# First attention of a two-layer trunk: norms of queries and keys over two token tiles, values straight from PSUM

## The chip, the cores and the metric

The kernel runs on one core of one Trainium2 chip. The metric is device microseconds of one execution, as the median of several runs: 2759.04 us for the kernel before (three runs, 2758.87 to 2761.37). The engines are named as the profile names them: PE is TensorE (matmuls; PEld its weight loads), DVE VectorE, ACT ScalarE, POOL GpSimd, and SP issues the DMAs.

## The reference, cut to what matters

Two transformer layers over 1024 latent tokens and 256 context tokens, model width 1024, 16 heads of 64. Layer 0 mixes by two-dimensional neighbourhood attention (the first attention), layer 1 by a sliding window with four key heads (the second attention); each layer ends with a gated feed-forward network. The change touches the norm of each head's query and key:

```python
def rmsnorm(x, g):
    x32 = x.astype(jnp.float32)
    y = x32 * lax.rsqrt(jnp.mean(x32 * x32, axis=-1, keepdims=True) + RMS_EPS)   # RMS_EPS = 1e-6
    return (y * g.astype(jnp.float32)).astype(x.dtype)

def attn_inputs(h, w_qkv, g_q, g_k, n_kv, with_q=True):
    y = h @ w_qkv
    q = rmsnorm(y[..., :D_MODEL].reshape(bsz, t, n_kv, N_HEADS // n_kv, HEAD_DIM), g_q)
    kv = y[..., D_MODEL:]
    k = rmsnorm(kv[..., :kv_w].reshape(bsz, t, n_kv, HEAD_DIM), g_k)   # over each head's 64 values
    v = kv[..., kv_w:].reshape(bsz, t, n_kv, HEAD_DIM)                 # not normed
    return q, k, v

def attend(q, k, v, bias=None, mask=None, sink=None):
    s = jnp.einsum('...qngd,...knd->...ngqk', q, k).astype(jnp.float32) * (HEAD_DIM ** -0.5)
    ...                                                                # + bias, mask; softmax p
    return jnp.einsum('...ngqk,...knd->...qngd', p.astype(v.dtype), v)
```

## The kernel before

The tokens lie in ten tiles of 128 (eight latent, two context). The first attention goes through eight head pairs. For each pair, `plan_na_qkv` (line 1084) plans one step per token tile, ten steps: eight groups of three matmuls give 384 columns in a PSUM bank `mm`: two heads of queries, two of keys, two of values. ScalarE copies all 384 columns to SBUF (`qraw`). `plan_rstd` (line 470) then makes the reciprocal root of the mean square of each of the four heads: ScalarE squares 256 columns (`qsq`), VectorE sums each head's 64 (`qv`), VectorE divides by 64 and adds the epsilon, GpSimd raises the four numbers to the power -1/2 (`qy`), and three small VectorE operations (`qt`, `qt`, `qy`) are a Newton step. VectorE scales queries and keys by it (`qn`). The values are copied from `qraw` by ScalarE or VectorE (`v`). Behind every second tile TensorE transposes the scaled queries and keys of both tiles (`pt<-idr,qn`), and ScalarE and VectorE split them in a high and a low part (`q`, `kkl`, `kll`; `kkc`, `klc` for the context).

`plan_na_su` plans the attention units on these: scores `s` on TensorE, a negated minimum with bias on VectorE (`S`, `m`), the exponential on ScalarE, the reciprocal of the sum (`sm`) and a scaling, transposes (`pt<-idr,S`) with copies back (`pt`), and the product with the values (`pv`, copied out as `osb`). The output projection of layer 0 follows (`woraw`, `whi`, `wlo` are its weights, `o2c`, `o0`, `o1` the split attention outputs, `oacc` its sums). The second attention (`plan_sw_qkv`, `plan_sw_ctx`) uses the same `plan_rstd`, with five and four heads a tile, and multiplies by rotary tables on VectorE or GpSimd (`qa`, `qb`).

The order on every engine is made by `Sched`. Each step is given to it with engines and an assumed duration, what it reads and writes, a key (earlier keys first), and which buffers it takes (`acq`) and gives back (`rel`). It plays the engines forward in time with these assumed durations and, whenever an engine is free, starts the ready step with the lowest key whose buffers are free; a step with two engines goes to the one that would finish it first. The instructions are then issued in that order, and on the chip each engine keeps it, waiting wherever an input is late. So a step that disappears, or another assumed duration, moves steps far from it, on every engine. The queries of pair `n` have the key `n`, the attention units `n + 5.5`; that is the distance by which projections run ahead. Two banks hold projections (`mm`), two `qraw` buffers.

All operations issued through this helper carry line 51 in the profile, so rows are told apart by the tiles that they write and read.

Of the kernel before, what the change touches and what calls it, by code (L numbers as in the profile page):

```python
# [11 lines left out]
F32 = mybir.dt.float32  # L12
# [5 lines left out]
P = 128  # L18
# [205 lines left out]
def trunk_kernel(ctx, tc, xtok, xseq, cc, crow, wmod, wmodt, bmod, gnorm, na_wqkv, na_gqk, na_bias, na_wo,  # L224
# [228 lines left out]
    def plan_qkv_mm(sc, key, psa, h, tt, slabs, s, J, c0=0, hkey=None):  # L453
# [3 lines left out]
        for kt in range(KT):  # L457
            def mm(e, kt=kt):
# [3 lines left out]
                for i, (a, w) in enumerate(((hh, wh), (hl, wh), (hh, wl))):  # L462
# [5 lines left out]
                  acq=[("mm", J["id"] + ("acc",), 1)] if kt == 0 else (), rel=[("w", i)] if kt % 2 else ())  # L468

    def plan_rstd(sc, key, J, c0, nh, wk, nsq):  # L470

        I = J["id"]

        def sq(e):
            J["sq"] = wk.tile([P, nsq], F32, tag="qsq", name="qsq", bufs=PTB["qsq"])
            act.activation(J["sq"][:, :nh * DH], J["raw"][:, c0:c0 + nh * DH], AF.Square)
        sc.op("act", t_act(nh * DH), sq, reads=[I + ("raw",)], writes=[I + ("sq",)], key=key, acq=[("qsq", I + ("sq",), 1)])

        def red(e):
            v = J["ms"] = tiny.tile([P, 5], F32, tag="qv", name="qv", bufs=4)  # L480
            dve.tensor_reduce(out=v[:, :nh], in_=J["sq"][:, :nh * DH].rearrange("p (h d) -> p h d", d=DH), axis=AX.X,
                              op=ALU.add)
        sc.op("dve", t_dve(nh * DH), red, reads=[I + ("sq",)], writes=[I + ("ms",)], key=key, rel=[I + ("sq",)])
# [6 lines left out]
        def pw(e):  # L490
            J["y"] = tiny.tile([P, 5], F32, tag="qy", name="qy", bufs=4)
            J["t"] = tiny.tile([P, 5], F32, tag="qt", name="qt", bufs=4)
            pool.tensor_tensor(out=J["y"][:, :nh], in0=J["ms"][:, :nh], in1=mhalf[:, :nh], op=ALU.pow)
        sc.op("pool", 0.42 + nh * 0.165, pw, reads=[I + ("ms",)], writes=[I + ("y",)], key=key)
        ny = lambda: (J["y"][:, :nh], J["t"][:, :nh], J["ms"][:, :nh])

        def newton(i):
            def f(e):
                y, t, v = ny()
                if i == 0:  # L500
                    dve.tensor_tensor(out=t, in0=y, in1=y, op=ALU.mult)
                elif i == 1:
                    dve.scalar_tensor_tensor(out=t, in0=t, scalar=-0.5, in1=v, op0=ALU.mult, op1=ALU.mult)
                else:
                    dve.scalar_tensor_tensor(out=y, in0=t, scalar=1.5, in1=y, op0=ALU.add, op1=ALU.mult)
# [3 lines left out]

# [543 lines left out]
    SBUFS, PTB = 5, dict(pt5=6, pt2=4, qsq=2)  # L1053
# [31 lines left out]
    def plan_na_qkv(n):  # L1085
# [7 lines left out]
        plan_qkv_mm(sc, key, psa, h, tt, slabs, hp, J, 0, ("h0", tt // 4) if hp == 0 else None)  # L1093

        def cp(e):
            J["raw"] = wk.tile([P, 384], F32, tag="qraw", name="qraw", bufs=2)
            act.activation(J["raw"], J["acc"][:, :384], AF.Copy)
        sc.op("act", t_actp(384), cp, reads=[K("acc")], writes=[K("raw")], key=key, acq=[("qraw", K("raw"), 2)],
              rel=[K("acc")])
# [1570 lines left out]
```

## Time and profile before

| | before |
|---|---|
| median of three runs | 2759.04 us (2758.87 to 2761.37) |
| span of the profiled execution | 2755.5 us, 42708 instructions |
| the profiled execution's own time | its span; the page gives none beyond it. The median is 3.5 us longer |
| PE / DVE / ACT / POOL busy | 2701.9 / 2247.1 / 1684.9 / 340.2 us |
| mean granted TensorE clock | 0.993 |
| first attention, projections and units | about 48 to 635 us |
| second attention | about 1620 to 2020 us |

Busy time is that of the records: matmul records overlap, so a TensorE that is busy throughout can still be waiting a little inside. The idle time of an engine is put down to what released it. The chain of waits follows the last instruction back to what released each step, and a share of it is time in which the end hung on that engine.

### The profile page before, as it was taken

The page shows a single profiled execution, that of the slowest core. Times are in us where ns is not written, and L with a number is a line of the kernel's source. Part 1 is how long each engine was busy: PE and PEld are TensorE (multiplying, and loading weights), DVE is VectorE, ACT ScalarE, POOL GpSimd, SP SyncE. Part 2 cuts the span into 40 slices and gives each one's busy share as a digit, 9 for nine tenths or more (in the row PEclk, how much of TensorE's full clock was granted, in tenths as well). Part 3 has the DMA queues.
Part 4 walks back from the last instruction along what each step waited for, and adds up shares of the span by engine and source line. Part 5 has one row for each costly group of instructions (what it writes and reads, how often), then busy time and mean ns, then how long its engine had stood idle before and what let it go on. Part 6 is the DMA issues. An engine that isn't in the chain of part 4 may idle for free.

```text
span 2755.5 us, 42708 instructions
## 1 busy us (share of the span) xinstructions
PE 2701.9 (98%) x15300; PEld 2282.4 (83%) x15300; DVE 2247.1 (82%) x4938; ACT 1684.9 (61%) x3000; POOL 340.2 (12%) x520
## 2 busy tenths in 40 slices
PE   7999999998999999999999999999999999999999
PEld 5999999987799988887888877777778788888887
DVE  5988888887778688787887889898877988888757
ACT  6777777776456555555564556666754666656443
POOL 1211111112000000000001007455410000000000
PEclk9999999999999999999999999999999999999999
DMA  7343343335656643334376562143243232334655
GB/s 263 98 127 117 117 135 119 111 96 165 216 170 184 184 142 104 129 118 135 119 249 198 188 201 68 43 129 102 78 152 113 88 115 100 112 107 146 234 175 186
DMA packets 147884, 387.89 MB, mean 141 GB/s; under 512 B 21332, under 2 KB 32084, under 8 KB 147288
## 3 DMA queue, kind: packets, MB, share of 16 engines
q1 hardware_dynamic: 147672, 385.17, 43.2%
q8 instruction: 120, 1.97, 0.3%
q14 instruction: 92, 0.75, 0.1%
HBM read 318.12 MB, written 66.99 MB: 140 GB/s over the span
## 4 chain that ended last, share of the span: by engine, by line
PE 76%; DVE 7%; DMA 2%; issue 2%; POOL 1%; ACT 1%; SPq 0%; DVEq 0%; ACTq 0%; POOLq 0%
PE ua L51 17%; PE uc L51 13%; PE dn L51 12%; PE mm L51 11%; PE pt L51 6%; PE oacc L51 4%; PE ud L51 4%; PE s L51 4%; PE dnc L51 2%; PE pv L51 2%; DVE S L51 1%; DVE wlo L51 1%; DMA woraw<-in_na_wo_dram 1%; DVE xn L51 1%; PE ug L51 0%
## 5 line engine op out<-in xcount | busy, mean ns | idle before, releaser
L51 ACT ACTIVATE whi<-wraw 128x512 fp32r<-128x512 f32 (+1 forms) x264 | 212.3, 804 | 153.6 <-PE uc L51 57.8
L51 DVE TENSOR_TENSOR wlo<-wraw,whi 128x512 fp32r<-128x512 f32 (+1 forms) x264 | 240.6, 912 | 47.7 <-ACT whi L51 47.3
L51 ACT ACTIVATE S<-S,m 128x640 f32<-128x640 f32 (+3 forms) x288 | 220.8, 768 | 63.2 <-DVE m L51 44.9
L51 PE MATMUL dn<-ghi,whi 128*128 128x512 f32 x616 | 240.0, 390 | 0.1
L51 PE MATMUL dn<-glo,whi 128*128 128x512 f32 x616 | 239.9, 389 | 0.2 <-DVE glo L51 0.2
L51 PE MATMUL dn<-ghi,wlo 128*128 128x512 f32 x616 | 239.8, 389 | 0.0
L51 ACT ACTIVATE whi<-s 128x1024 fp32r<-128x1024 f32 (+1 forms) x118 | 110.9, 941 | 182.1 <-PE uc L51 107.7
L51 POOL TENSOR_TENSOR qy<-qv,mhalf 128x4 f32<-128x4 f32 (+1 forms) x114 | 135.3, 1188 | 597.3 <-DVE qv L51 572.1
L51 PE MATMUL pt<-idr,S 128*128 128x128 f32 x1288 | 193.8, 277 | 11.9 <-DVE S L51 4.2
L51 PEld LDWEIGHTS pt<-idr,S 128*128 128x128 f32 x1288 | 151.5, 141 | 45.8 <-issue 12.0
L51 ACT ACTIVATE ghi<-graw 128x512 fp32r<-128x512 f32 x154 | 95.7, 628 | 144.5 <-PE dn L51 85.9
L51 PE MATMUL mm<-whi,h0hi 128*128 128x384 f32 x512 | 180.1, 352 | 0.0
L51 ACT ACTIVATE pt<-pt 128x512 f32<-128x512 f32 (+2 forms) x259 | 133.4, 535 | 64.6 <-PE pt L51 62.7
L51 PE MATMUL mm<-wlo,h0hi 128*128 128x384 f32 x512 | 172.1, 336 | 0.0
L51 DVE TENSOR_TENSOR glo<-graw,ghi 128x512 fp32r<-128x512 f32 x154 | 105.6, 695 | 78.1 <-ACT ghi L51 48.4
L51 DVE TENSOR_TENSOR wlo<-s,whi 128x1024 fp32r<-128x1024 f32 (+1 forms) x118 | 126.9, 1077 | 21.2 <-ACT whi L51 20.8
L51 PEld LDWEIGHTS dn<-ghi,whi 128*128 128x128 f32 x616 | 115.7, 188 | 24.6 <-issue 0.5
L51 PEld LDWEIGHTS dn<-glo,whi 128*128 128x128 f32 x616 | 115.7, 188 | 24.2 <-DVE glo L51 0.5
L51 PE MATMUL ua<-t12hi,whi 128*128 128x512 f32 x344 | 134.8, 392 | 0.9 <-ACT c L51 0.9
L51 PEld LDWEIGHTS dn<-ghi,wlo 128*128 128x128 f32 x616 | 115.6, 188 | 24.0
L51 PE MATMUL ua<-t12lo,whi 128*128 128x512 f32 x344 | 134.0, 390 | 0.0
L51 PE MATMUL ua<-t12hi,wlo 128*128 128x512 f32 x344 | 133.9, 389 | 0.0
(372 smaller groups left out, 8305.2 us busy)
## 6 DMA issues: line engine op xcount, KB each, us to landing
wraw<-in_w_up_dram SPq DMA_DIRECT2D x133, 512.0 KB, 3.8
wmt<-in_wmodt_dram SPq DMA_DIRECT2D x96, 512.0 KB, 4.0
wraw<-in_w_down_dram SPq DMA_DIRECT2D x44, 512.0 KB, 3.7
graw<-g_dram SPq DMA_DIRECT2D x44, 512.0 KB, 4.8
wraw<-in_w_down_dram SPq DMA_DIRECT2D x88, 256.0 KB, 3.0
graw<-g_dram SPq DMA_DIRECT2D x66, 256.0 KB, 2.8
wm<-in_wmod_dram SPq DMA_DIRECT2D x32, 512.0 KB, 6.7
slab<-in_na_wqkv_dram SPq DMA_DIRECT2D x32, 384.0 KB, 3.2
```

The costliest lines, as they stand in the source:

```text
L51: r = f(*a, **k)
```

## The change

Six edits. The mean is folded in the square, whose input is scaled by 64 to the power -1/2, so that the sum of squares is the mean already. The epsilon moves from VectorE to GpSimd, where it is added just in front of the power, as part of the same planned step. The Newton step multiplies in another order, with as many operations. In the first attention the copy of each tile takes the 256 columns of queries and keys alone, in one half of a buffer for two tiles. The values are copied from the PSUM bank, which so has two users (`uses=2`). And behind every second tile one norm over eight heads and one scaling of 512 columns take the place of two of each. `qsq` has one buffer of 512 columns in place of two of 256; `qraw` has two buffers for two tiles each. The second attention gets the first three edits through `plan_rstd`.

```diff
-    def plan_rstd(sc, key, J, c0, nh, wk, nsq):
+    def plan_rstd(sc, key, J, nh, wk, nsq, src, reads=None):
         I = J["id"]
+        n = nh * DH
         def sq(e):
             J["sq"] = wk.tile([P, nsq], F32, tag="qsq", name="qsq", bufs=PTB["qsq"])
-            act.activation(J["sq"][:, :nh * DH], J["raw"][:, c0:c0 + nh * DH], AF.Square)
+            act.activation(J["sq"][:, :n], src(), AF.Square, scale=DH ** -0.5)
...
-        def mean(e):
-            v = J["ms"][:, :nh]
-            dve.tensor_scalar(out=v, in0=v, scalar1=1.0 / DH, scalar2=EPS, op0=ALU.mult, op1=ALU.add)
-        sc.op("dve", t_dve(0), mean, reads=[I + ("ms",)], writes=[I + ("ms",)], key=key)
         def pw(e):
-            pool.tensor_tensor(out=J["y"][:, :nh], in0=J["ms"][:, :nh], in1=mhalf[:, :nh], op=ALU.pow)
-        sc.op("pool", 0.42 + nh * 0.165, pw, reads=[I + ("ms",)], writes=[I + ("y",)], key=key)
+            v = J["ms"][:, :nh]
+            pool.tensor_scalar(out=v, in0=v, scalar1=EPS, scalar2=None, op0=ALU.add)
+            pool.tensor_tensor(out=J["y"][:, :nh], in0=v, in1=mhalf[:, :nh], op=ALU.pow)
+        sc.op("pool", 0.55 + nh * 0.165, pw, reads=[], writes=[I + ("ms",), I + ("y",)], key=key)
...
@@ def plan_na_qkv(n):
-            act.activation(J["raw"], J["acc"][:, :384], AF.Copy)
-        sc.op("act", t_actp(384), cp, reads=[K("acc")], writes=[K("raw")], key=key, acq=[("qraw", K("raw"), 2)], rel=[K("acc")])
-        plan_rstd(sc, key, J, 0, 4, wk, 256)
+            if tt % 2 == 0:
+                f["raw", pr] = wk.tile([P, 2, 256], F32, tag="qraw", name="qraw", bufs=2)
+            act.activation(f["raw", pr][:, tt % 2, :], J["acc"][:, :256], AF.Copy)
...
-            copy(e, f["v"][tt], pair(J["raw"][:, 256:384]))
+            copy(e, f["v"][tt], pair(J["acc"][:, 256:384]))
...
         if tt % 2 == 0:
             return
+        both = [two + ("raw", 0), two + ("raw", 1)]
+        plan_rstd(sc, key, J, 8, wk, 512, lambda: f["raw", pr].rearrange("p a b -> p (a b)"), both)
+        def qn(e):
+            f["qn", pr] = wk.tile([P, 2, 256], F32, tag="qn", name="qn", bufs=2)
+            hd = lambda a: a.rearrange("p a (h d) -> p (a h) d", d=DH)
+            ENG[e].tensor_tensor(out=hd(f["qn", pr]), in0=hd(f["raw", pr]), in1=J["y"].unsqueeze(2).to_broadcast([P, 8, DH]), op=ALU.mult)
+        sc.op("dve", t_dve(512), qn, reads=both + [K("y")], writes=[two], key=key, acq=[("qn", two, 1)], rel=[two + ("raw",)])
```

What this does to the order, at three places. On ScalarE in the middle of the first attention, the copy and norm of one projected tile before (`S` and `sm` are the softmax of a unit, `pt` a copy of its transposes):

```order
L51 ACTIVATE qraw<-mm 128x384
L51 ACTIVATE qsq<-qraw 128x256
L51 ACTIVATE pt_5003<-pt 128x512
L51 ACTIVATE v<-qraw 128x128
L51 ACTIVATE S<-S,sm 128x512
L51 ACTIVATE S,sm<-S,m_5021 128x256
```

and now the second tile of a pair, with the square of both tiles:

```order
L51 ACTIVATE qraw<-mm 128x256
L51 ACTIVATE v<-mm 128x128
L51 ACTIVATE pt_4518<-pt 128x512
L51 ACTIVATE qsq<-qraw 128x512
L51 ACTIVATE S,sm<-S,m_4511 128x640
L51 ACTIVATE pt_4547<-pt 128x512
```

The value copy moved in front, to the bank that it now reads, and the square stands once per pair.

On VectorE at the end of the first attention, the last Newton step and scaling of the last pair before (`ISA` with `m` and `bias` is the biased minimum of a unit):

```order
L51 TENSOR_TENSOR qt<-qy 128x4
L51 TENSOR_SCALAR S,m_8580<-s 128x256
L51 SCALAR_TENSOR_TENSOR qt<-qt,qv 128x4
L51 RECIPROCAL sm<-sm 128x1
L51 SCALAR_TENSOR_TENSOR qy<-qt,qy 128x4
L51 TENSOR_SCALAR S<-S,sm 128x640
L51 TENSOR_TENSOR qn<-qraw,qy 128x256
```

and now:

```order
L51 TENSOR_TENSOR qt<-qv,qy 128x8
L51 ISA S,m_8074<-s,bias,m_8074 128x384
L51 ISA m_8074 128x1
L51 SCALAR_TENSOR_TENSOR qt<-qt,qy 128x8
L51 RECIPROCAL sm<-sm 128x1
L51 SCALAR_TENSOR_TENSOR qy<-qt,qy 128x8
L51 TENSOR_TENSOR o0lo_8092<-osb,o0hi_8088 128x8x16
L51 TENSOR_TENSOR o1lo_8097<-osb,o1hi_8093 128x8x16
L51 TENSOR_TENSOR qn<-qraw,qy 128x512
```

One such sequence serves both tiles of the pair, and two splits of an attention output that GpSimd did before stand inside it.

On GpSimd at the same place, before:

```order
L51 TENSOR_TENSOR wlo<-slab,whi 128x768
L51 TENSOR_TENSOR qy<-qv,mhalf 128x4 x70
L51 TENSOR_TENSOR wlo<-woraw,whi 128x1024
L51 TENSOR_TENSOR qy<-qv,mhalf 128x4
L51 TENSOR_TENSOR o0lo_8626<-osb,o0hi_8622 128x8x16
L51 TENSOR_TENSOR o1lo_8631<-osb,o1hi_8627 128x8x16
```

and now:

```order
L51 TENSOR_SCALAR qv<-qv 128x8
L51 TENSOR_TENSOR qy<-qv,mhalf 128x8
L51 TENSOR_TENSOR wlo<-woraw,whi 128x1024
L51 TENSOR_TENSOR o1lo_8094<-oraw,o1hi_8093 128x512
L51 TENSOR_TENSOR o0lo_8089<-oraw,o0hi_8088 128x512
L51 TENSOR_TENSOR o1lo_8094<-oraw,o1hi_8093 128x512
```

The weight subtraction `wlo<-woraw` stood in front of the last power and now stands behind it.

## Rows read from the trace of the kernel before

**Rows 1.** page, busy time of the engines (us, share of the span, instructions)
```profile
PE 2701.9 (98%) x15300; PEld 2282.4 (83%) x15300; DVE 2247.1 (82%) x4938; ACT 1684.9 (61%) x3000; POOL 340.2 (12%) x520
```

**Rows 2.** windows: stretch, us, busy us of PE, PEld, DVE, ACT, POOL; clock; DMA
```profile
60.00:600.00 540.00, 536.68 (x3687) 493.11 (x3685) 472.48 (x1657) 401.82 (x946) 83.97 (x74) 1.00 0.36 114
620.00:630.00 10.00, 6.87 (x30) 5.25 (x31) 8.98 (x35) 6.66 (x14) 2.82 (x2) 0.67 0.52 165
630.00:640.00 10.00, 8.19 (x66) 6.70 (x62) 8.36 (x23) 7.90 (x19) 1.89 (x3) 0.99 0.41 120
1640.00:1980.00 340.00, 335.87 (x2296) 262.48 (x2296) 307.95 (x1021) 230.61 (x514) 187.61 (x362) 1.00 0.25 77
```

**Rows 3.** chain of waits from 264 to 600 us: shares by line, and one piece
```profile
by line: PE mm L51 46.3%; PE pt L51 15.2%; PE pv L51 13.7%; PE s L51 11.8%; DVE kll L51 1.6%; DVE S L51 1.4%; issue 1.4%; DMA wmt<-in_wmodt_dram 1.3%; DVE q L51 1.2%; DVE wlo L51 1.1%; ACT kkl L51 0.9%; ACT q L51 0.8%; DVE wmt L51 0.7%; ACT
473.40 4.71 PE mm L51 x27
```

**Rows 4.** what PE waited for from 48 to 640 us: the first and the last kind
```profile
PE pt L51 <- DVE S L51: 1.5, 1, 1.5
PE pt L51 <- ACT pt L51: 0.5, 2, 0.3
```

**Rows 5.** groups by shape, 48 to 640 us: busy us, mean ns | idle before
```profile
L51 ACT ACTIVATE qraw<-mm 128x384 f32<-128x384 f32 x80 | 38.9, 486 | 20.0 <-PE mm L51 18.4 <-DVE sm L51 0.5 <-DVE qn L51 0.4
L51 ACT ACTIVATE qsq<-qraw 128x256 f32<-128x256 f32 x80 | 33.1, 414 | 1.6
L51 DVE TENSOR_TENSOR qn<-qraw,qy 128x256 f32<-128x256 f32 x80 | 33.5, 420 | 0.4
L51 DVE TENSOR_REDUCE qv<-qsq 128x4 f32<-128x256 f32 x80 | 32.7, 410 | 3.0 <-ACT qsq L51 2.5
L51 DVE TENSOR_SCALAR qv<-qv 128x4 f32<-128x4 f32 x80 | 12.8, 161 | 0.2
L51 DVE TENSOR_TENSOR qt<-qy 128x4 f32<-128x4 f32 x80 | 14.3, 179 | 4.6 <-POOL qy L51 3.9
L51 DVE SCALAR_TENSOR_TENSOR qy<-qt,qy 128x4 f32<-128x4 f32 x80 | 12.6, 158 | 0.5
L51 ACT ACTIVATE v<-qraw 128x128 f32<-128x128 f32 x43 | 12.8, 298 | 0.0
L51 DVE COPY v<-qraw 128x128 f32<-128x128 f32 x37 | 8.1, 220 | 2.6 <-ACT qraw L51 2.3
```

**Rows 6.** the same view: other operations of the widths that the change adds
```profile
L51 ACT ACTIVATE osb<-pv 128x256 f32<-128x256 f32 x27 | 10.3, 382 | 20.4 <-PE pv L51 20.3
L51 ACT ACTIVATE pt<-pt 128x128 f32<-128x128 f32 x15 | 4.1, 273 | 1.3 <-PE pt L51 1.1
L51 DVE COPY pt<-pt 128x128 f32<-128x128 f32 x15 | 4.3, 288 | 1.7 <-PE pt L51 1.5
```

**Rows 7.** page, costliest groups: two 512-wide operations of ScalarE and VectorE
```profile
L51 ACT ACTIVATE ghi<-graw 128x512 fp32r<-128x512 f32 x154 | 95.7, 628 | 144.5 <-PE dn L51 85.9
L51 DVE TENSOR_TENSOR glo<-graw,ghi 128x512 fp32r<-128x512 f32 x154 | 105.6, 695 | 78.1 <-ACT ghi L51 48.4
```

**Rows 8.** GpSimd in order of time: powers of two and four columns
```profile
8.80 0.71 POOL L51 TENSOR_TENSOR o2y<-o2v,mhalf 128x2 f32<-128x2 f32 x1 [7.49 <-DVE o2v L51]
15.26 1.01 POOL L51 TENSOR_TENSOR o0y<-o0v,mhalf 128x4 f32<-128x4 f32 x1 [5.75 <-DVE o0v L51]
```

**Rows 9.** in order of time, 619 to 623 us: GpSimd, VectorE, TensorE (start, us)
```profile
619.45 2.36 POOL L51 TENSOR_TENSOR wlo<-woraw,whi 128x1024 fp32r<-128x1024 f32 x1
...
619.98 1.86 DVE L51 TENSOR_TENSOR qt<-qy 128x4 f32<-128x4 f32 x1
...
622.24 0.44 PE L51 MATMUL s<-kkl,q 128*128 128x384 f32 x1 [1.39 <-DVE S L51]
```

**Rows 10.** groups by shape, second attention, 1640 to 1980 us
```profile
L51 DVE TENSOR_SCALAR qv<-qv 128x5 f32<-128x5 f32 x31 | 8.1, 261 | 0.1
L51 POOL COPY S<-small 128x1 f32<-128x1 f32 x110 | 27.4, 273 | 1.6 <-ACT S L51 1.6
```

More of the change, by code (lines that the diff above doesn't have):

```diff
@@ L451, in plan, with plan_qkv_mm @@
                   writes=[("wl", i)], key=key - 2, rel=[("raw", i)])
-    def plan_qkv_mm(sc, key, psa, h, tt, slabs, s, J, c0=0, hkey=None):
+    def plan_qkv_mm(sc, key, psa, h, tt, slabs, s, J, c0=0, hkey=None, uses=1):
         hh, hl = h[tt // 4]
@@ L479, in red @@
         def red(e):
[L480 to L483, printed above, removed]
-        def mean(e):
-            v = J["ms"][:, :nh]
-            dve.tensor_scalar(out=v, in0=v, scalar1=1.0 / DH, scalar2=EPS, op0=ALU.mult, op1=ALU.add)
@@ L488, in plan_rstd @@
[L488 to L495 removed]
+            v = J["ms"] = tiny.tile([P, 8], F32, tag="qv", name="qv", bufs=4)
@@ new lines, in red, with pw @@
+            dve.tensor_reduce(out=v[:, :nh], in_=J["sq"][:, :n].rearrange("p (h d) -> p h d", d=DH), axis=AX.X, op=ALU.add)
+        sc.op("dve", t_dve(n), red, reads=[I + ("sq",)], writes=[I + ("ms",)], key=key, rel=[I + ("sq",)])
+        def pw(e):
+            J["y"] = tiny.tile([P, 8], F32, tag="qy", name="qy", bufs=4)
+            J["t"] = tiny.tile([P, 8], F32, tag="qt", name="qt", bufs=4)
+            v = J["ms"][:, :nh]
+            pool.tensor_scalar(out=v, in0=v, scalar1=EPS, scalar2=None, op0=ALU.add)
+            pool.tensor_tensor(out=J["y"][:, :nh], in0=v, in1=mhalf[:, :nh], op=ALU.pow)
@@ L1092, in plan_na_qkv @@
         f = F.setdefault(hp, dict(q=[None] * NT, v=[None] * NT))
-        plan_qkv_mm(sc, key, psa, h, tt, slabs, hp, J, 0, ("h0", tt // 4) if hp == 0 else None)
+        plan_qkv_mm(sc, key, psa, h, tt, slabs, hp, J, 0, ("h0", tt // 4) if hp == 0 else None, 2)
+        pr = tt // 2
+        two = ("qnp", hp, pr)
         def cp(e):
-            J["raw"] = wk.tile([P, 384], F32, tag="qraw", name="qraw", bufs=2)
-            act.activation(J["raw"], J["acc"][:, :384], AF.Copy)
-        sc.op("act", t_actp(384), cp, reads=[K("acc")], writes=[K("raw")], key=key, acq=[("qraw", K("raw"), 2)],
-              rel=[K("acc")])
-        plan_rstd(sc, key, J, 0, 4, wk, 256)
+            if tt % 2 == 0:
+                f["raw", pr] = wk.tile([P, 2, 256], F32, tag="qraw", name="qraw", bufs=2)
+            act.activation(f["raw", pr][:, tt % 2, :], J["acc"][:, :256], AF.Copy)
+        sc.op("act", t_actp(256), cp, reads=[K("acc")] + ([two + ("raw", 0)] if tt % 2 else []), writes=[two + ("raw", tt % 2)],
+              key=key, acq=[("qraw", two + ("raw",), 1)] if tt % 2 == 0 else (), rel=[K("acc")])
         def vhi(e):
             f["v"][tt] = fin.tile([P, 2, DH], F32, tag="vc" if cx else "v", name="v", bufs=4 if cx else 8)
-            copy(e, f["v"][tt], pair(J["raw"][:, 256:384]))
+            copy(e, f["v"][tt], pair(J["acc"][:, 256:384]))
         vk, qk = ("v", hp, tt), ("q", hp, tt)
@@ L1128, in tr @@
                 pe.transpose(pt[:, i * P:(i + 1) * P], f["qn", pr][:, i % 2, i // 2 * P:(i // 2 + 1) * P], idf)
-        sc.op("pe", 0.44, tr, reads=[two + (0,), two + (1,)], writes=[K("pt")], key=key, acq=[("pt", K("pt"), 8)], rel=[two])
+        sc.op("pe", 0.44, tr, reads=[two], writes=[K("pt")], key=key, acq=[("pt", K("pt"), 8)], rel=[two])
         kx = ("kkc", hp) if cx else ("kk", pr)
@@ L2390, in plan_sw_qkv @@
               rel=[K("acc")])
-        plan_rstd(sc, key, J, c0, nh, wk, 320)
+        plan_rstd(sc, key, J, 5, wk, 320, lambda: J["raw"][:, :320])
         vk, qk = ("v", g, tt), ("q", g, tt)
```

30 lines of the change are left out of this document (11 added, 19 removed).

## The prediction

> **What bounds the kernel now.** I read the page first [rows 1]. TensorE is busy for 98% of the span, VectorE for 82%, ScalarE for 61% and GpSimd for 12%; the reader is to see that the change takes work from the second busiest engine and none from the busiest. An average over stages says little, so the table by stage came next [rows 2]. In the body of the first attention (60 to 600 us) TensorE is idle for 540.00 - 536.68 = 3.3 us only, while VectorE is busy for 472.48 of 540 (87%) and ScalarE for 401.82 (74%). At its end (620 to 640 us), where the projections of the last head pair no longer fill TensorE, 3.1 and 1.8 us are idle, and in 620 to 630 the granted clock is 0.67, so a part of that slice ran at 1.2 GHz in place of 2.4. The second attention (1640 to 1980 us) leaves TensorE 4.1 us idle, with VectorE at 307.95 of 340 (91%).
>
> A busy TensorE record can hide waiting, so the chain of waits was third [rows 3]: from 264 to 600 us it lies on TensorE for 46.3 + 15.2 + 13.7 + 11.8 = 87% and elsewhere for 13%, which is 44 us, mostly pieces of VectorE and ScalarE of about 1% each. Last came what TensorE itself waited for [rows 4]: six kinds of wait from 48 to 640 us, none above 1.5 us, together 7.2 us. Between 7 us of waits and 44 us of chain lies what faster norms can give back in this stage; everything else in it is TensorE's own work, of which the change removes none.
>
> **The change part by part.** First attention, per pair of token tiles, on VectorE [rows 5]: before, two each of reduce, mean, three Newton steps and scaling, 2 x (0.410 + 0.161 + 0.179 + 0.158 + 0.158 + 0.420) = 2.97 us (the second Newton step reads like the third, which is shown). After, one of each without the mean. A 512-wide two-input operation took 0.695 us [rows 7], 0.275 more than the 256-wide scaling; the reduce gets the same addition, 0.410 + 0.275 = 0.685 (its bounds are 0.410 and 0.820). The tiny steps keep their durations at eight columns. Sum: 0.685 + 0.495 + 0.695 = 1.87 us. Saved: 1.10 us x 40 pairs = 44 us.
>
> On ScalarE: two copies of 384 and two squares of 256, 2 x (0.486 + 0.414) = 1.80 us, become two copies of 256 from PSUM (0.382, as the output copy took) and one square of 512 (0.628, as another 512-wide activation took), 1.39 us [rows 5 to 7]. Saved: 0.41 x 40 = 16 us.
>
> The values were copied from SBUF by ScalarE 43 times (0.298) and VectorE 37 times (0.220) [rows 5]. Now, by the order, ScalarE does 60 and VectorE 20, from PSUM. For ScalarE 0.273 is the bound below, from the 128-wide evacuation [rows 6], and 0.298 the one above; I take 0.273, since it reads the same memory. So ScalarE gets 60 x 0.273 - 43 x 0.298 = +3.6 us. For VectorE I take 0.288, by the same kind of row [rows 6]: 20 x 0.288 - 37 x 0.220 = -2.4 us. What it may cost is elsewhere: the accumulator bank is now held until the value copy as well. In the order more than half of ScalarE's 60 value copies are the very next row behind the query-key copy, and there are two banks, so the next user of the same one stands a whole projection of 24 matmuls away (4.2 us at the 0.174 below). I cost it at nothing; without that cover a tile waits for one operation more, 0.273 us or, behind a 512-wide one, 0.9.
>
> The order also reshuffles: VectorE is handed 11 more of the 512-wide evacuations, and loses 13 casts and 7 softmax scalings to ScalarE. At the two-input rows that is 11 x 0.695 - 13 x 0.420 - 7 x 0.695 = -2.7 us, too little to weigh. In all VectorE falls by about 49 us, from 87% to some 79% of the body, and ScalarE by about 10.
>
> GpSimd's power took 0.71 us on two columns and 1.01 on four [rows 8], so 0.15 a column and 1.62 on eight, plus an addition that no row shows. Its bounds are the one-column copy, 0.273 [rows 10], and the two-column power, 0.71; I take 0.273, the simpler operation. 40 x 1.89 = 76 us against 80 x 1.01 = 81: GpSimd gets no heavier here.
>
> The chain of a pair, behind its second tile's matmuls, gets longer: before 0.486 + 0.414 + 0.410 + 0.161 + 1.01 + 0.495 + 0.420 = 3.4 us, after 0.382 + 0.628 + 0.685 + 0.273 + 1.62 + 0.495 + 0.695 = 4.8. What hides it is TensorE's own queue. Counted in the order, the fewest matmuls between a pair's last projection and its transposes are 41 (before 30), the median 66 (before 65); at 4.71 / 27 = 0.174 us for each projection matmul [rows 3], 41 are 7.1 us at most. The transposes are placed far enough behind.
>
> Gain in the body: the bounds are the whole off-path chain, 44 us, and a loss that is the slower rival below. I take 5 us, since the idle time of the records (3.3) and the sum of waits (7.2) are the rows that measure TensorE itself, and a VectorE with a fifth of its time free instead of an eighth should end most of those waits, as five of the six kinds are waits for VectorE.
>
> End of the stage. The longest waits of TensorE stand here: 1.39 us at 622.24 behind a VectorE softmax piece [rows 9]. That piece was late because the Newton step in front of it, normally 0.179 us, took 1.86 us from 619.98, just while GpSimd ran its 2.36 us subtraction from 619.45 [rows 9]. In the changed order GpSimd does its last power first and that subtraction after it, and the pair's norm needs one pass instead of two. I take 3 us of the 4.9 idle; bounds 8.2 us (with the 3.3 that the clock took in 620 to 630) and -2 (the longer chain of the last pair).
>
> The Trainium skill ("SBUF — State Buffer", section Who interferes with whom) says that GpSimd and VectorE share one port pair as an exclusive lock and that a VectorE instruction with two SBUF inputs blocks against a GpSimd instruction that reads SBUF. The 1.86 us agree. It speaks against moving VectorE work to GpSimd, as the addition is moved here: by it the second attention below would give nothing, and the sum would be 8 us and 2751.
>
> Second attention: the shared helper drops the mean from VectorE, 31 x 0.261 = 8.1 us there, and adds an addition on GpSimd, 31 x 0.273 = 8.5 us [rows 10]. One operation replaces another in the same serial chain, and by the order four rotary products go to VectorE and four leave GpSimd. Bounds: 8.1 us gained, if VectorE alone sets the stage, and 8.5 lost, if each addition lies on the path. TensorE's idle 4.1 us [rows 2] is the nearer row; I take 1 us gained.
>
> Sum: 5 + 3 + 1 = 9 us off the profiled span, 2755.5 to 2746.5. The page gives no time for that execution beyond its span; the median of the three timed runs, 2759.04, is 3.5 us longer, and I carry that over: 2750.
>
> **The rivals.**
> No change: TensorE is the bound and its records already stand back to back. Idle time of 3.3 us in 540 and weight loads busy for 493.11 of 540 [rows 2] speak for it; against it the 13% of the chain and the waits at the end. It gives 0 to 4 us, some 2757. The Trainium skill ("Perfetto Trace Analysis", Identifying the Most-Contended Engine) would optimise the engine with the highest occupancy first and judge TensorE by its weight loads; on those 91% it would expect little here, and the trace so far bears it out.
>
> Larger gain: most of the 44 us of off-path chain is real lateness. With VectorE's queue shorter, half of it goes: 2759 - 22 - 4 = 2733. Against it: waits of 7.2 us in all [rows 4].
>
> Slower: the pair's chain. A pair's norm starts only when both tiles are copied, and every VectorE piece queued ahead delays a chain that is 1.4 us longer. If that reaches the transposes at the eight tightest of the 40 pairs, TensorE stands 8 x 1.4 = 11 us, and one such stop may bring the slower clock, 3.3 us as in 620 to 630, with the scores and softmax of that pair queued behind. Together 14 us, less 4 from the other two stages: 2769. It decides from a VectorE queue of about 7.1 - 4.8 = 2.3 us ahead of the chain.
>
> Second attention slower: the order there is planned anew, GpSimd is busy for 187.61 of 340 [rows 2], and its rotary products wait behind each added operation. 8.5 us lost there, 5 gained before: 2762.
>
> **How the numbers follow.** Forecast 0.46, its own range 2745 to 2753. No change 0.28, larger gain 0.08, slower by the chain 0.09, slower in the second attention 0.09. A measurement tells 0.2%, 5.5 us, from no change: below 2753.5 is faster. Faster 0.46 + 0.08 = 0.54; same 0.28 and half of the last case, which ends within 5.5 us, 0.32; slower 0.14. For 8 in 10 the range takes in the no-change case and the second attention's loss: 2742 to 2763.
>
> **What would show it.** Right: VectorE busy near 430 us from 60 to 600, one 512-wide reduce near 0.69, powers near 1.6, TensorE's waits below 4 us, the granted clock above 0.67 where the projections end. Wrong: TensorE idle in front of the query-key transposes or of the first scores of a pair; a projection waiting for a value copy; a power or an addition so slow that VectorE idles behind it; or a stage that ends when it did although VectorE has 49 us less.

## The result: 0.25% slower, and the profile after

The changed kernel takes 2765.8 us (median of ten runs) against 2758.9 for the kernel before (ten runs): ratio 1.0025, interval 1.0016 to 1.0034. The forecast was 2750. The page of the changed kernel, busy time of the engines (us, share of the span of 2764.7 us, instructions), against [rows 1]:

```profile
PE 2700.3 (98%) x15300; PEld 2281.5 (83%) x15300; DVE 2233.2 (81%) x4625; ACT 1673.0 (61%) x2971; POOL 334.5 (12%) x542
```

The same windows as [rows 2], of the changed kernel:

```profile
60.00:600.00 540.00, 534.96 (x3662) 491.38 (x3660) 457.59 (x1384) 390.38 (x924) 75.75 (x74) 1.00 0.37 114
620.00:630.00 10.00, 9.37 (x64) 7.25 (x63) 9.31 (x31) 9.79 (x20) 2.01 (x3) 1.00 0.37 111
630.00:640.00 10.00, 5.47 (x31) 4.96 (x30) 9.46 (x19) 6.51 (x16) 2.21 (x1) 0.78 0.36 118
1640.00:1980.00 340.00, 331.56 (x2260) 259.56 (x2260) 304.52 (x1002) 231.00 (x505) 190.18 (x376) 0.99 0.26 80
```

VectorE is busy for 15 us less in the body of the first attention and ScalarE for 11, yet TensorE gets through fewer matmuls there (3662 for 3687) and idles 5.0 us in place of 3.3. The hole at the end of the stage has moved from 620 to 630 into 630 to 640. In the second attention TensorE idles 8.4 us in place of 4.1.

Operations of the changed kernel from 48 to 640 us by shape (busy us, mean ns), against [rows 5 to 8]:

```profile
L51 POOL TENSOR_TENSOR qy<-qv,mhalf 128x8 f32<-128x8 f32 x40 | 68.6, 1715 | 3.3
...
L51 ACT ACTIVATE qraw<-mm 128x256 f32<-128x256 f32 x80 | 30.2, 378 | 9.3 <-PE mm L51 8.2
...
L51 DVE TENSOR_TENSOR qn<-qraw,qy 128x512 f32<-128x512 f32 x40 | 27.6, 689 | 0.5
...
L51 DVE TENSOR_REDUCE qv<-qsq 128x8 f32<-128x512 f32 x40 | 27.3, 682 | 1.9 <-ACT qsq L51 1.7
...
L51 ACT ACTIVATE qsq<-qraw 128x512 f32<-128x512 f32 x40 | 25.1, 626 | 0.3
...
L51 ACT ACTIVATE v<-mm 128x128 f32<-128x128 f32 x60 | 16.1, 268 | 0.0
...
L51 POOL TENSOR_SCALAR qv<-qv 128x8 f32<-128x8 f32 x40 | 13.0, 325 | 527.7 <-DVE qv L51 385.3 <-DVE sm L51 142.4
```

The durations are those of the prediction within 0.02 us, but for GpSimd's power (1.715 for 1.62) and addition (0.325 for 0.273) and the first Newton step (0.220 in the mean, for 0.179). GpSimd's two are 0.15 us a pair heavier than they were taken to be, 6 us over the 40 pairs if nothing covered them; the other durations hold, so the failure isn't in them.

What TensorE waited for from 48 to 640 us in the changed kernel (total, times, longest), against [rows 4]:

```profile
PE pt L51 <- DVE pt L51: 4.2, 2, 3.9
PE pt L51 <- DVE S L51: 1.4, 4, 0.6
PE pt L51 <- DVE qn L51: 1.1, 2, 0.7
```

All kinds together are 9.6 us, before 7.2. The 3.9 us is one stop at the end of the stage, in front of the last pair's query-key transposes. GpSimd, VectorE and TensorE there in order of time (start, us, [idle before]), against [rows 9]:

```profile
628.23 1.67 POOL L51 TENSOR_TENSOR qy<-qv,mhalf 128x8 f32<-128x8 f32 x1
...
629.86 2.35 POOL L51 TENSOR_TENSOR wlo<-woraw,whi 128x1024 fp32r<-128x1024 f32 x1
629.92 2.31 DVE L51 TENSOR_TENSOR qt<-qv,qy 128x8 f32<-128x8 f32 x1 [0.18 <-POOL qy L51]
...
632.69 0.16 DVE L51 SCALAR_TENSOR_TENSOR qt<-qt,qy 128x8 f32<-128x8 f32 x1
632.77 0.15 DVE L51 RECIPROCAL sm<-sm 128x1 f32<-128x1 f32 x1
...
632.88 0.17 DVE L51 SCALAR_TENSOR_TENSOR qy<-qt,qy 128x8 f32<-128x8 f32 x1
632.97 0.28 DVE L51 TENSOR_TENSOR o0lo<-osb,o0hi 128x128 fp32r<-128x128 f32 x1
...
633.37 0.69 DVE L51 TENSOR_TENSOR qn<-qraw,qy 128x512 f32<-128x512 f32 x1
...
634.71 0.66 PE L51 MATMUL pt<-idr,qn 128*128 128x128 f32 x4 [3.93 <-DVE pt L51]
```

The collision of before is there again: GpSimd does its last power first and the subtraction right behind it, and the Newton step is released by that same power, so the two start together and both last 2.3 us. The four rows from 632.69 show a second thing: small VectorE records of 0.15 to 0.17 us start 0.08 to 0.11 us apart, so they overlap, and a small operation taken out may give back only about half of its record.

What TensorE waited for from 1640 to 2080 us, first before, then after:

```profile
PE pt L51 <- DVE S L51: 2.0, 3, 1.3
PE pt L51 <- ACT o0hi L51: 1.8, 1, 1.8
PE pt L51 <- ACT pt L51: 1.0, 3, 0.6
PE pt L51 <- POOL qa L51: 1.0, 1, 1.0
```

```profile
PE pt L51 <- DVE S L51: 6.8, 7, 1.7
PE pt L51 <- POOL qa L51: 3.3, 5, 1.2
PE pt L51 <- ACT S L51: 1.5, 1, 1.5
PE pt L51 <- DVE pt L51: 1.4, 1, 1.4
```

Most of the growth is in two kinds that were there before: softmax pieces and rotary products stop TensorE more often. By the ends of TensorE's matmuls in the two traces, the lateness of 9.2 us in the span comes from the body of the first attention (2.7 at the last projection), its end, the output projection and the first feed-forward (together 1.2), and the second attention (6.2); the last feed-forward gives 0.9 back. The medians differ by 7.0 us only. In every run of the changed kernel the time is 1.8 us above the span; by the same 1.8 the profiled execution of before took 2757.3, 1.6 below its median, and that of the changed kernel, 2766.5, was 0.7 above. So some 2 us of these shares belong to the two executions, not to the change.

### The profile page after: what moved, and what is told of

It is laid out like the page before. It is cut to its first block, busy times and chain, and to the rows that moved or that the text cites. A ratio compares the mean times of both kernels' runs of the same rounds, so it can differ in the third digit from the quotient of the medians.

```text
span 2764.7 us, 42384 instructions
## 1 busy us (share of the span) xinstructions
PE 2700.3 (98%) x15300; PEld 2281.5 (83%) x15300; DVE 2233.2 (81%) x4625; ACT 1673.0 (61%) x2971; POOL 334.5 (12%) x542
## 4 chain that ended last, share of the span: by engine, by line
PE 65%; DVE 6%; POOL 2%; issue 2%; DMA 1%; ACT 1%; SPq 0%; DVEq 0%; POOLq 0%; ACTq 0%
PE ua L51 17%; PE dn L51 13%; PE uc L51 13%; PE pt L51 5%; PE mm L51 5%; PE oacc L51 4%; PE ud L51 4%; PE dnc L51 2%; PE s L51 2%; DVE S L51 1%; DVE wlo L51 1%; POOL qa L51 1%; POOL qb L51 1%; DVE xn L51 1%; POOL qy L51 1%
## 5 line engine op out<-in xcount | busy, mean ns | idle before, releaser
L51 ACT ACTIVATE pt<-pt 128x512 f32<-128x512 f32 (+2 forms) x243 | 125.5, 537 | 76.0 <-PE pt L51 75.1
L51 PE MATMUL mm<-whi,n1lo 128*128 128x384 f32 x384 | 128.8, 335 | 0.0
```

Source lines behind the costliest of these rows:

```text
L51: r = f(*a, **k)
```

## Experiments: parts of the change

**The mean of the second attention back on VectorE.** The old helper is kept beside the new one and called by the second attention alone, which so has the order of before (one of its two calls is shown):

```diff
-        plan_rstd(sc, key, J, 5, wk, 320, lambda: J["raw"][:, :320])
+        plan_rstd_dve(sc, key, J, c0, nh, wk, 320)
```

> The changed kernel with the shared norm helper of before (mean on VectorE, power alone on GpSimd) in the second attention, so that this stage is planned and ordered as before; the first attention stays as changed. In the changed kernel TensorE ends the first attention's score products 3.4 us later and the whole program 9.3 us later than before, so some 6 us are lost inside the second attention. Theory A (the second attention loses by the helper's new division of work, in whatever way): its stage comes back to before, time falls by 5 to 7 us to 2759 to 2761, and what is left over before is the 3 to 4 us of the first attention. Rival B (the second attention is only late because of what the first hands over, or its traces differ by chance from run to run): time stays at 2764 to 2767.

Measured 2760.3 us, ratio 1.0009 (1.0001 to 1.0018): A by the time. The second attention (end of the first feed-forward to the end of the first up projections of the second) lasts 526.9 us, in the changed kernel 530.7, before 524.5, so 3.8 of the 6.2 us come back in this profile. The kernels below that hold the old order of this stage give about 524 to 526.6, so 526.9 is the high end of what that order shows.

**GpSimd's addition left out, the order held.**

```diff
-            pool.tensor_scalar(out=v, in0=v, scalar1=EPS, scalar2=None, op0=ALU.add)
```

> The changed kernel without GpSimd's addition of 1e-6 to the mean squares (this part of the computation is left out) in both attentions; the order on TensorE, VectorE and ScalarE stays the same row for row. Theory A1 (the added operation itself is on the path in the second attention, 34 of them at 0.37 us = 12.6 us at most): second attention 4 to 7 us shorter than in the changed kernel, first attention 1 to 2 us shorter, time 2758 to 2761. Rival A2 (the new order of the second attention costs, not the operation): second attention within 2 us of the changed kernel, time 2763 to 2766.

Measured 2761.9, ratio 1.0011 (1.0002 to 1.0020), between the two: 4 of the 7 us come back although the order is held. In the second attention A2 holds: it lasts 529.9 us, and four kernels with this order and the addition 530 to 532, so the operation is worth about 1 us of the some 5 lost there, no more than the four differ among themselves. In the first attention the addition is on the path: the projections end at 620.2 for 622.7. Matmul by matmul the two traces part mainly at four places: transposes of qn at 261 and 500 us (0.7 and 0.9 us) and of softmax pieces at 342 and 418 (0.5 and 0.4). A1 had expected the reverse shares, 4 to 7 us in the second attention and 1 to 2 in the first.

**The values alone.** The kernel before, with this part of the change in the first attention:

```diff
-            act.activation(J["raw"], J["acc"][:, :384], AF.Copy)
+            act.activation(J["raw"], J["acc"][:, :256], AF.Copy)
...
-            copy(e, f["v"][tt], pair(J["raw"][:, 256:384]))
+            copy(e, f["v"][tt], pair(J["acc"][:, 256:384]))
```

> The kernel before with one part of the change alone: in the first attention the values are copied straight from PSUM and the copy of queries and keys is 256 wide; norms stay per tile with the mean on VectorE, the second attention is untouched. Theory C (the longer chain of pair norms costs the first attention its 3.4 us): no change, 2756 to 2760, TensorE's score products end where they did before within 1 us. Rival D (holding the accumulator for the value copy costs): score products end 2 to 4 us later than before, 2761 to 2763.

Measured 2759.0, ratio 1.0010 (1.0001 to 1.0019). The score products, here the products of the softmax with the values (`pv`), end 5.9 us later, more than either expected, but the output projection gives 3.4 of it back. What it shows is a new order with stops elsewhere (5.5 us of scores behind softmax maxima, `m`). It can't separate C from D, and led to the question what an order alone is worth.

## Experiments: the same work in other orders

The planner simulates each operation with the price it is told. One price, that of GpSimd's power (with the addition, in the changed kernel), is altered; no operation of the work changes. Steps that two engines can do also move between them (the old work issues 4937 to 4970 instructions on VectorE over the five prices and 2975 to 3007 on ScalarE), so "order" stands here for order and engine:

```diff
-        sc.op("pool", 0.55 + nh * 0.165, pw, reads=[], writes=[I + ("ms",), I + ("y",)], key=key)
+        sc.op("pool", 0.80 + nh * 0.165, pw, reads=[], writes=[I + ("ms",), I + ("y",)], key=key)
```

> The changed kernel with the planner told 0.80 + 0.165 a column for GpSimd's addition and power in place of 0.55 + 0.165 a column: in the trace the two took 0.37 + 1.25 = 1.62 us at five columns (told: 1.375, now 1.625) and 0.325 + 1.715 = 2.04 at eight (told: 1.87, now 2.12). Same work, other order. Theory A2 (the order costs, because it is planned on too short a time of GpSimd): 3 to 7 us faster than the changed kernel, 2759 to 2763, most of it in the second attention. Theory A1 (the operation costs): within 2 us of the changed kernel, 2764 to 2768. A change of 3 us or more to the slower side would show that an order by itself is worth as much as the whole loss.

> The changed kernel with the planner told 0.65 + 0.165 a column for GpSimd's addition and power (0.55 in the changed kernel: 2766 us; 0.80: 2752 us). Same work, a third order. Theory O (the order decides by chance: which operation stands next to which at the ends of the stages; the told price is only a die that is thrown again): no trend, the time lies anywhere from 2750 to 2768. Theory H (the told price has to be near the measured one, and the closer the better): halfway, 2757 to 2762.

> The changed kernel with the planner told 0.95 + 0.165 a column, 0.15 above what the trace shows for the two operations. Theory O: anywhere from 2750 to 2768, not tied to 0.80's 2752. Theory H: within 3 us of the 0.80 kernel, 2750 to 2755, since 0.80 and 0.95 stand about equally far from the measured sums (1.62 at five columns, 2.04 at eight).

> Control: the kernel before, not one instruction of its work changed, with the planner told 0.55 + 0.165 a column for GpSimd's power in place of 0.42 + 0.165 (at five columns 1.375 told against 1.366 measured; before: 1.245). Theory O (order chance): the time moves by 3 to 10 us to either side of 2757, with most of it at the ends of the two attentions. Rival N (an order alone is worth less than 3 us, so the change's 8 us are its work): 2755 to 2760.

> Control: the kernel before with the planner told 0.70 + 0.165 a column for the power (1.525 told at five columns, 0.16 above the measured time). Theory O: moves by 3 to 10 us to either side of 2757, not in line with the 0.55 control. Rival N: 2755 to 2760.

> A third control: the kernel before with the planner told 0.80 + 0.165 a column for the power. Theory O (chance of the order; the order of before, at 0.42, happens to be a good one, since 0.55 gave 2764 and 0.70 gave 2767): 2757 to 2768, on average 2763, so more likely slower than before than not. Rival (the told price of 0.80 is in itself good, as it was for the changed kernel at 2752): 2750 to 2755.

> The changed kernel with the planner told 0.42 + 0.165 a column, the price the kernel before was planned with; a fifth order of the same work. Theory O (work and order apart: the changed work averages below the old work over orders, by some 5 to 8 us, and single orders scatter by 5 to each side): 2750 to 2766, its mean with the other four below 2760. Rival (the changed work is really slower and 0.80 and 0.95 were lucky): above 2762.

> The changed kernel with the planner told 0.70 + 0.165 a column; a sixth order. Theory O: 2750 to 2766, not slower than the control of the old work at 0.70 (2767). Rival: above 2762.

> A fourth control: the kernel before with the planner told 0.95 + 0.165 a column for the power. Theory O (the order of before is the best of its kind by luck or choice): 2759 to 2770, slower than before at 0.42. Rival (the old work has orders as good as before's as often as not): 2757 or less.

> The changed kernel at 0.80 + 0.165 a column once more, on the chip of the hybrid beside it. Theory O (an order is a property of the program, not of the run): 4 to 6 us faster than before again, 2751 to 2753. Rival (chance of the runs): within 2 us of before.

Times of this table in us, medians of 4 to 11 runs. They come from several chips, on which the kernel before took 2755.9 to 2758.9, so the ratios, each to the kernel before beside it, are what is compared. The three stage columns are read from one profiled execution each (end of the last projection of the first attention, end of its output projection, length of the second attention):

| work, told price | median | ratio to before (interval) | projections end | output projection ends | second attention |
|---|---|---|---|---|---|
| old, 0.42 (before) | 2757 | 1 | 620.0 | 776.8 | 524.5 |
| old, 0.55 | 2764.0 | 1.0030 (1.0018 to 1.0042) | 623.3 | 781.7 | 527.0 |
| old, 0.70 | 2766.7 | 1.0038 (1.0023 to 1.0053) | 622.8 | 781.2 | 528.9 |
| old, 0.80 | 2769.5 | 1.0052 (1.0037 to 1.0067) | 628.0 | 782.3 | 531.8 |
| old, 0.95 | 2759.6 | 1.0012 (1.0003 to 1.0021) | 624.0 | 776.6 | 527.1 |
| new, 0.42 | 2762.1 | 1.0018 (1.0009 to 1.0027) | 621.4 | 776.0 | 531.7 |
| new, 0.55 (the change) | 2765.8 | 1.0025 (1.0016 to 1.0034) | 622.7 | 781.3 | 530.7 |
| new, 0.65 | 2759.8 | 1.0016 (1.0007 to 1.0026) | 619.1 | 774.4 | 528.1 |
| new, 0.70 | 2759.2 | 1.0013 (1.0003 to 1.0022) | 619.3 | 778.6 | 530.7 |
| new, 0.80 | 2752.0 | 0.9981 (0.9972 to 0.9990) | 620.6 | 773.2 | 527.6 |
| new, 0.80 again | 2752.9 | 0.9985 (0.9976 to 0.9994) | 619.8 | 769.3 | 527.6 |
| new, 0.95 | 2754.6 | 0.9991 (0.9982 to 1.0001) | 621.1 | 773.0 | 527.3 |

Three readings.

An order alone moves this kernel by 0.5%: the old work spans 1.0000 to 1.0052. Rival N falls with the first two controls, and the repeated run shows that a good order lasts. Two expectations were missed: the new work at 0.80 came out 7 us faster than A2's range (2759 to 2763), and the old work at 0.80 is 1.5 us slower than O's (2757 to 2768). The new work at 0.42, 2762.1, stands in O's range and just in its rival's (above 2762). O's ranges are 11 to 18 us wide, so that the others fit them says little by itself.

By work, the five old orders average 1.0026 and the six new ones 1.0007: the new work is 0.19% or 5 us *faster* over orders, with a standard error of 0.12% from their scatter. By stages, the projections end at 623.6 on average with the old work and 620.7 with the new, and the second attention lasts 527.9 and 529.4. That is the right direction for the first attention and a small loss in the second, but at 1.6 standard errors it isn't settled.

The shipped orders are an uneven pair: the old work stood in the best of its five, the new in the worst of its six. For that there is a theory that fits better than chance alone, H: the traces give the power 1.12 us at four columns (mean of 80; 1.01 in most) and 1.37 at five, where 0.42 tells 1.08 and 1.25; with the addition they give 2.04 at eight and 1.62 at five, where the change tells 1.87 and 1.38, since it prices the addition at 0.13 and it takes 0.33 to 0.37. The new work's first attention is shortest at 0.65 and 0.70 (0.72 would match), its second at 0.80 and 0.95 (0.80 would match). H was not refuted by 0.65 and 0.95, both inside its ranges; but 0.70 and 0.80 differ by 7 us, old 0.55 matches five columns almost exactly and is 2.5 us worse there than 0.42, and old 0.95 breaks the trend. How much is price and how much luck stays open.

Where such an order loses its time is read from what TensorE waited for, 600 to 720 us, in the old work at 0.55 and at 0.95:

```profile
PE mp L51 <- DVE nsum L51: 4.1, 1, 4.1
PE mm L51 <- DVE wlo L51: 2.1, 2, 1.3
PE s L51 <- DVE S L51: 1.4, 1, 1.4
```

```profile
PE pt L51 <- DVE kll L51: 3.5, 1, 3.5
PE s L51 <- DVE qt L51: 1.9, 1, 1.9
PE pt L51 <- DVE sm L51: 1.6, 1, 1.6
```

Single stops of 1 to 4 us, each order with others, at the ends of the stages where little is left to put in front of them.

## Experiments: single suspects, the order held

**The subtraction beside the Newton step.** One instruction moved to VectorE:

```diff
             def lo(e):
+                e = "dve" if self.shared and self.l == 0 else e
```

> The changed kernel with one instruction moved: the subtraction wlo of the first output projection that GpSimd runs for 2.35 us from 629.86 is issued at the same place of the order on VectorE, just ahead of the first Newton step of the last pair, which took 2.31 us from 629.92 (0.22 elsewhere) and behind which TensorE stood for 3.93 us. Everything else keeps its order. Theory L (the Newton step is slow only because that GpSimd subtraction runs beside it): the step is back at 0.2 us, VectorE pays 1.2 us for the subtraction instead, the stop falls by about 1.1 us to 2.8, and the last query-key transposes come 1 us earlier. Rival (the step is slow for itself, or because the power is late): the step keeps 2 us and, behind 1.2 us more work, the stop grows to 5.

In order of time in this kernel:

```profile
629.94 1.22 DVE L51 TENSOR_TENSOR wlo<-woraw,whi 128x1024 fp32r<-128x1024 f32 x1
...
631.07 0.16 DVE L51 TENSOR_TENSOR qt<-qv,qy 128x8 f32<-128x8 f32 x1
...
633.71 0.66 PE L51 MATMUL pt<-idr,qn 128*128 128x128 f32 x4 [2.65 <-DVE pt L51]
```

L holds in its numbers: the step is back at 0.16 us, the stop falls from 3.93 to 2.65. The time, 2762.1, has the ratio 1.0028 (1.0016 to 1.0040), which can't tell 1 us from nothing; the last product with the values ends 1.3 us earlier. The 2.65 us that are left show that the collision was only a part of this stop.

**More work on VectorE**, behind the scaling of each pair, or ahead of it inside the pair's chain:

```diff
+            dve.tensor_tensor(out=f["raw", pr], in0=f["raw", pr], in1=f["raw", pr], op=ALU.max)
```

> The changed kernel with VectorE work added in the first attention, outside the chain of a pair: behind each of the 40 scalings (qn) an operation of two inputs and 512 columns that changes nothing that is used later, 40 x 0.69 = 28 us; the planner isn't told, so the order of everything else stays. Theory V (what VectorE has to do sets the body of this stage, as the prediction's 5 us for 49 us of work assumed): the projections end 3 us later than in the changed kernel (625.5). Theory O (it doesn't; single places in the order do): within 1 us of 622.7.

> The same operation, 40 x 0.69 us on VectorE, but inside the chain of a pair, ahead of the scaling qn (it leaves the values as they are). Theory C (a pair's longer chain reaches TensorE at a few of the 40 pairs, as the transposes of qn at 261 and 500 us do by about 1 us each in the changed kernel): each such place costs 0.7 us more, and the projections end 1.5 to 4 us later than in the kernel with the same load outside the chain. Rival (the 41 and more matmuls in front of the transposes cover the chain at all pairs): the same as that kernel within 0.7 us.

Measured 2775.2, ratio 1.0072 (1.0056 to 1.0089), and 2774.3, ratio 1.0069 (1.0054 to 1.0084). The body from 60 to 600 us (columns as in [rows 2]) with the load outside the chain, and TensorE's first two kinds of wait from 48 to 640 us:

```profile
60.00:600.00 540.00, 529.35 (x3617) 484.37 (x3617) 474.52 (x1397) 383.89 (x910) 73.76 (x72) 1.00 0.36 114
```

```profile
PE pt L51 <- DVE S L51: 4.1, 6, 1.3
PE pt L51 <- DVE qn L51: 1.9, 3, 0.8
```

The same two views with the load inside the chain:

```profile
60.00:600.00 540.00, 528.90 (x3609) 482.68 (x3608) 472.17 (x1396) 383.29 (x909) 72.96 (x72) 1.00 0.36 113
```

```profile
PE pt L51 <- DVE qn L51: 4.5, 6, 1.5
PE pt L51 <- DVE S L51: 2.1, 4, 0.6
```

The projections end 8.9 and 9.6 us later than in the changed kernel. Of this, 1.0 and 0.9 us stand already at 55 us, before the first added operation at 56 (the kernel with the old second attention is 0.85 late there without any load), so the load costs 7.9 and 8.7: far above what V expected (3), and O falls here. In the time it is some 12 us, against the kernel of the moved subtraction on the same chip. That is 0.28 us at the end of the stage for each microsecond of VectorE. The chain adds 0.7 to that, C's lower bound being 1.5, so C falls: inside the chain TensorE stops at the transposes of qn, outside at those of softmax pieces, for as long (all waits together 10.5 and 10.8 us). No query-key copy waits for the buffer that the added operation reads (`qraw` waits for TensorE alone in both). What counts is VectorE's queue, not the pair's chain.

**Less work on VectorE**, in the kernel before and its order:

```diff
-            act.activation(J["sq"][:, :nh * DH], J["raw"][:, c0:c0 + nh * DH], AF.Square)
+            act.activation(J["sq"][:, :nh * DH], J["raw"][:, c0:c0 + nh * DH], AF.Square, scale=DH ** -0.5)
-            dve.tensor_scalar(out=v, in0=v, scalar1=1.0 / DH, scalar2=EPS, op0=ALU.mult, op1=ALU.add)
+            pass
```

> The kernel before in its own order, row for row, with one piece of the change's saving: the division by 64 goes into the square's scale and the mean's VectorE operation is gone in both attentions, 80 x 0.161 and 33 x 0.261 us; the addition of 1e-6 is left out. Theory V (less VectorE work is worth time where the order stays: 28 us more work cost 9 us, 0.32 a microsecond): 13 us less give 4 us at the end of the first attention's projections and 8.6 us less give 2.7 in the second, 2750 to 2753. Theory O2 (a plan is laid out for its own durations: more than planned costs, less than planned gives nothing): within 2 us of before, 2755 to 2759.

Measured 2753.5, ratio 0.9989 (0.9980 to 0.9997). The time lies half a microsecond above V's range (2750 to 2753) and below O2's; the place is not V's. Body and a stretch of the output projection, this kernel:

```profile
60.00:600.00 540.00, 536.85 (x3688) 493.34 (x3687) 467.52 (x1584) 401.39 (x946) 85.31 (x74) 1.00 0.36 114
664.00:700.00 36.00, 32.51 (x190) 28.42 (x186) 19.48 (x30) 15.01 (x24) 0.50 (x1) 0.95 0.78 267
700.00:720.00 20.00, 20.00 (x92) 16.40 (x93) 19.50 (x37) 11.18 (x18) 0.70 (x1) 1.00 0.83 304
```

The last of these windows in the kernel before:

```profile
700.00:720.00 20.00, 18.66 (x79) 15.41 (x80) 18.20 (x36) 10.95 (x18) 0.70 (x1) 0.91 0.77 277
```

The projections end at 620.1 for 620.0, the second attention lasts 525.2 for 524.5: nothing gained in either stage where the means stood. The 2.9 us come at 700, where neither kernel has a mean: one stop of TensorE in front of the feed-forward's norm is 0.6 us in place of 3.0, and the granted clock behind it 1.00, where before it was 0.91, a part of the window at 1.2 GHz after the stop. Two executions of one program can differ at just this place: in the two profiles of the new work at 0.80 the same stop is 1.8 and 1.4 us, the granted clock from 697 to 702 us 0.66 and 1.00, and 2 us arise there. So why the time fell stays open. VectorE's busy time fell by 5 us in the body, not by the 11 that the records taken out there add up to; at 0.28 a microsecond 5 us would be worth 1.4, an estimate, and the two profiles of 0.80 differ by 0.8 at the end of the projections. So this run can't say that less VectorE work is worth less than more of it costs.

**The best of both**: first attention of the change at 0.80, second attention of before.

> The first attention of the changed kernel in its order at 0.80 (its score products ended at 666.0 and the second attention began at 1612.3, 5.6 us ahead of before) with the second attention of before: mean on VectorE, told 0.42, its old order (1617.9 to 2142.4 = 524.5 us in before, 526.6 and 526.9 in two other kernels that hold it; 527.6 in the 0.80 kernel). If stages add up (theory O, orders of the two attentions are independent): 0 to 3 us faster than the 0.80 kernel, 2749 to 2752. Rival (what the first stage gains is lost again behind it): 2755 or more.

Measured 2749.6, ratio 0.9977 (0.9968 to 0.9986), the fastest kernel of the study, beside 0.9985 (0.9976 to 0.9994) for the 0.80 kernel on the same chip. Its windows, over the end of the first attention and over the second:

```profile
664.00:780.00 116.00, 113.80 (x606) 97.41 (x603) 79.91 (x131) 51.69 (x76) 4.06 (x4) 1.00 0.63 212
1640.00:1980.00 340.00, 335.85 (x2302) 260.92 (x2303) 306.84 (x1028) 232.58 (x520) 190.53 (x370) 1.00 0.25 77
```

The second attention has its 335.85 us of TensorE back (335.87 in [rows 2]). The stages' gains add up: run side by side on one chip, eleven times each, the two kernels have means of 2749.7 and 2752.5 us, 2.8 apart with 1.8 either way.

## Why the prediction was wrong

**The failed step is the one that weighed the reshuffled order at nothing** ("11 x 0.695 - 13 x 0.420 - 7 x 0.695 = -2.7 us, too little to weigh"). It counted what the order gives VectorE to do, not where TensorE then stops. Orders of unchanged work differ by up to 0.52%, 14 us, here; the whole forecast was 9. With it failed the step that put a pair's chain out of TensorE's reach ("The transposes are placed far enough behind"): in this order GpSimd's added operation reaches TensorE, and without it 4 of the 7 us come back. At 0.80 the same operation stands in a kernel 5 us faster than before, so order and operation can't be priced apart.

**Body, 5 us gained: came out 2.7 lost.** 2.5 of that is the added GpSimd operation, by the kernel without it, which reaches TensorE mainly at four places. In this order the waits of TensorE from 60 to 600 us went from 2.9 to 4.5 us in place of ending. The size was too large by the prediction's own rows as well: TensorE idles 3.3 us there, and of the 7.2 us of waits 4.3 stand at the end of the stage, one in [rows 9] and these two, where the next term counts them again:

```profile
625.13 2.06 PE L51 MATMUL pt<-idr,S 128*128 128x128 f32 x8 [1.50 <-DVE S L51]
...
634.50 0.39 PE L51 MATMUL mm<-o2clo,whi 128*128 128x256 f32 x1 [1.37 <-DVE o2clo L51]
```

Over orders the new work ends the body 2.9 us earlier, so the sign of the term may have been right for the work and was wrong for this order.

**VectorE 49 us lighter: 15.** The sum took records at full length. From 60 to 600 us they add up to 37 us less, but the busy time falls by 15, as small records overlap their neighbours. ScalarE's 10 came out as 11.

**More VectorE work costs 0.28 us a microsecond; what less of it gives isn't settled.** The argument that a freer VectorE "should end most of those waits" was not borne out: over orders the waits from 48 to 640 us are 8.7 us on average with the old work and 7.5 with the new, and without the means the stage ends where it did. But the means were only 5 us of busy time. The Trainium skill ("Perfetto Trace Analysis", Identifying the Most-Contended Engine) would optimise the engine of the highest occupancy first, and judge TensorE by its weight loads: 491.38 of 540 us in the changed kernel's body, 91%, against VectorE's 85%. The trace agrees that TensorE comes first, yet there 28 us more work for VectorE cost 8 us.

**End of the stage, 3 us gained: nothing.** From the last projection to the last pair's transposes TensorE takes 12.0 us, before 11.9. The collision was read rightly and its removal wrongly. That GpSimd does the power before the subtraction is just what makes them collide with the Newton step that waits for the power, and it was so before too: the power of the tile that collided ran from 618.48 for 1.01 us, right in front of the subtraction at 619.45. The Trainium skill ("SBUF — State Buffer", Who interferes with whom) has a VectorE operation with two SBUF inputs and a GpSimd one that reads SBUF block each other at a shared port. The traces agree: the Newton step ends 0.02 us behind the subtraction in the changed kernel (632.23 and 632.21) and 0.03 before (621.84 and 621.81), and takes 0.16 us without it.

**Second attention, 1 us gained: 5 to 6 lost.** The rival named this stage and the fresh plan of it, but priced the additions (8.5). They are worth about 1 us; most of the rest is the order, since giving the stage its old helper and order brings it to 526.9 us in one kernel and back to about 524 in the hybrid.

**The pair's chain as a rival** is worth 0.7 us in 28 of added chain; TensorE's other matmuls cover it at nearly all pairs, as predicted. They don't at the last pair, where the stop of 3.93 us stands, and in the body of the changed kernel TensorE stops three times in front of `qn` transposes, together for 1.8 us.

**Values from PSUM** were rightly costed at about nothing here: in the changed kernel no projection matmul waits for a value copy, in its other orders one waits 0.3 us at most, and in the kernel with the values alone two wait 1.2 and 0.5 us.

Of the signs that it named, VectorE's 430 us came out as 458 and the waits below 4 us as 9.6; of those of being wrong, the query-key transposes and the stage that ends no earlier came.

## What to carry to other kernels

Where a planner or a table sets the order, a change of work is a new order too: time the old work in a few other orders first, and take no gain smaller than their scatter for real before the new work has been tried in a few as well. A new operation gets its price from the trace, here 0.33 to 0.37 us, not 0.13. And where two engines collide, ask what releases each: here both operations stood behind the same power and started within 0.1 us.

## Unexpected in the hardware

GpSimd's five-column addition took longer in the second attention (0.370 us) than the eight-column one in the first (0.325). Where projections fill TensorE, stage ends repeat within 0.3 to 0.8 us from one profiled execution to another (622.7, 622.9 and 623.0 us for three kernels with the same order up to there; 620.6 and 619.8 for two executions at 0.80). In the output projection they repeat badly: at 0.80 it ended at 773.2 and 769.3, and half of that arose at one stop of TensorE and the clock behind it, at 697 to 702 us.
